# Weights stationary, input moving: one 512-column matmul over the input's high and low halves in place of two of 256 columns

## The chip, the cores and the metric

The kernel runs on one core of a Trainium2 chip. The metric is the device time of one execution in microseconds, given as the median of several runs. A core has a matrix engine (TensorE; PE in the profile, its weight loads PEld), a vector engine (VectorE, DVE), a scalar engine (ScalarE, ACT), GpSimd (POOL) and SyncE (SP), from whose queue the transfers from memory are issued here. Each engine works through its own list of instructions in order and waits for the others through semaphores. Matmul results are written to PSUM, which has eight banks of 512 float32 per partition; everything else lives in SBUF.

## The reference

One layer of a bidirectional encoder over 256 positions of width 2048. The input is normalised and multiplied by one wide matrix; its columns are cut into parts that feed two branches and their gates:

```python
h = _rms_norm(x, norm_g)
proj = jnp.einsum('bsd,dn->bsn', h, w_in.astype(h.dtype))
q_p, k_p, v_p, o_p, za_p, gif_p, xb_p, zb_p, ga_p, gb_p = jnp.split(proj, cuts, axis=-1)
ya = _mlstm_branch(q_p, k_p, v_p, o_p, za_p, gif_p, b_if, head_g)
yb = _rglru_branch(xb_p, zb_p, conv_w, conv_b, w_rg, b_rg, lam)
ya = jnp.einsum('bsw,wd->bsd', ya, w_branch_a.astype(ya.dtype))
yb = jnp.einsum('bsw,wd->bsd', yb, w_branch_b.astype(yb.dtype))
merged = (jax.nn.sigmoid(ga_p) * ya + jax.nn.sigmoid(gb_p) * yb).astype(x.dtype)
return x + jnp.einsum('bsd,de->bse', merged, w_out.astype(x.dtype))
```

A final normalisation follows. The first branch (mLSTM) has four heads with gated scores between queries and keys; the second (RG-LRU) has a short convolution along the sequence (the `xb` part), gates, and a linear recurrence run forwards and backwards; its result is multiplied by silu of the `zb` part.

## The kernel before

**High and low halves.** Every float32 operand of a large product is split in two: a high half, rounded to the matmul's input type (`F32R`), and a low half, the rounding's remainder. A product is then three matmuls: high by high, high by low, low by high. The normalised input (without its row factor, which is applied later: `rstd` as a column, `rbc` as a row) is held transposed, features on the partitions, as `hhi` (slot `H`) and `hlo` (slot `L`): 16 feature tiles of 256 positions each. `x_piece` (line 169) fills them two tiles at a time.

**Weights in chunks.** A block is 512 columns of a weight matrix, 2048 rows deep. It comes in eight chunks of 512 KB. `load_chunk` (line 96) issues the transfer on SP into one of five `raw` tiles, has ACT round it to `whi` (line 108, "the cast") and DVE subtract to get `wlo` (line 109, "the subtraction"). There are three pairs of `whi` and `wlo`, so the cast of a chunk can start when PE has finished the chunk three places before it.

**Two kinds of block.** `block_nat` (line 112) holds the input stationary and moves 512 columns of weights; its result has positions on the partitions. `block_tr` (line 128) holds 128 x 128 of the weights stationary and moves the input's 256 positions; its result has features on the partitions. For each of the 16 feature tiles k and each of four column groups m it issues three matmuls (lines 142 to 144): high weights by `hhi`, high weights by `hlo`, low weights by `hhi`. Two column groups share a bank, so a block fills a pair of banks; `pacc` has four single banks, so two pairs. `block_tr` serves 12 blocks: Q0, K0, Q1, K1 (the digit is the loop's index; K's results are also multiplied by `rbc`, line 388), XB0 to XB3 and ZB0 to ZB3. 31 blocks go through `block_nat`, three of them in the last projection.

**Order of the work.** Q0, K0, Q1, K1 come first. Then for each j in 0 to 3: `rg_block(j)` (XBj, its multiply by `rbc` into the padded tile `xp` on line 455, and the convolution on DVE on lines 461 to 468), followed by `head(j)` with three `block_nat` blocks V, O and Z. Then ZB0 to ZB3, then the gates and the branches' projections, and the output. Small steps hang in two queues. `tick()` (line 81), called ahead of each chunk, takes one step from each; `drain()` takes all that are left, `drain_to(fn)` all up to one step. In the queues are: the loads of x for the row factor (`r_load`), the row factor itself (`r_sum`, `r_row`, the latter a matmul of a diagonal and a copy to `rbc`), the gates (`g_...`), the score products (`s_mul`, `s_tr`), the recurrence's gate products (`unit`), exponentials (`decay`), roots (`root`) and scans (`scan`, lines 515 to 525), and a head's mixing and transposes (`mix`, `fin`). The steps of block XBj that are left after `head(j)` run during XB(j+1), those of XB3 during ZB0: one `root` and two `scan`.

A scheduler places the instructions on each engine's list from this order, with a cost model of its own. What stands under `urgent()` goes ahead of what doesn't: weight chunks and the emptying of PSUM are urgent, the convolution, scans, `fin` and `mix` are not.

## Time and profile before

| | |
|---|---|
| time, 3 runs | median 1053.61 us, 1052.96 to 1053.88 |
| span of the profiled execution, first to last instruction | 1050.9 us |
| mean granted TensorE clock of the span | 0.998 |
| transfers of weight chunks of `wi` | 255 of 512 KB and 2 of 256 KB |
| memory read and written | 196.32 MB, 2.10 MB; 189 GB/s over the span |
| GpSimd's busiest line, 673 (scales `fgs`, once) | 10.6 us |

The profile is of one execution; the runs' times are of others, and include what lies before the first and after the last instruction. The page gives the busy time of each engine as a share of the span, the chain of work that ended last, and groups of instructions by line. In a line of a group, the first number behind the bar is the group's busy time, the second the mean duration of one in ns, the last the time that the engine sat idle just before them, with what ended it. In a line of the timeline, the first number is the start in us from the span's start, the second the time to the end of the piece, then engine, line, operation, the tiles written and read, and how many instructions are merged in the piece; in brackets stands idle time before it. A matmul's duration includes the pipeline that it shares with its neighbours, so the distance between starts says what one costs. Windows give start and end, length, busy time of PE, PEld, DVE, ACT and POOL, clock, and what the transfers did.

### The profile page before, as it was taken

How to read it: one execution, taken by the hardware profiler on the slowest of the kernel's cores; microseconds unless marked ns; L12 is line 12 of the kernel's file. 1: busy time of each engine (PE TensorE's matmuls, PEld its weight loads, DVE VectorE, ACT ScalarE, POOL GpSimd, SP SyncE). 2: the span in 40 equal slices, each digit the busy share in tenths (PEclk: the TensorE clock that was granted, in tenths of full speed). 3: DMA queues.
4: the chain of work that ended last, by engine and by line, in shares of the span. 5: the costliest groups of instructions: out<-in, count | busy, mean ns of one | idle time of the engine just before them, and what ended most of it. 6: DMA issues, size and time to landing. Idle time of an engine off the chain costs nothing.

```text
span 1050.9 us, 14840 instructions
## 1 busy us (share of the span) xinstructions
PE 1039.4 (99%) x5876; PEld 914.9 (87%) x5876; DVE 646.9 (62%) x809; ACT 533.5 (51%) x689; POOL 36.7 (3%) x48
## 2 busy tenths in 40 slices
PE   9999999999999999999999999999999999999996
PEld 8999988898889888988999988888888888888886
DVE  6566785489549845974786654454454545545573
ACT  7535447765684658466644443434434344444461
POOL 2000000010001001000320000000000000000000
PEclk9999999999999999999999999999999999999999
DMA  9744545556655654664656556666666565667652
GB/s 339 254 158 143 180 159 185 163 182 198 196 161 167 198 197 160 187 214 161 200 181 184 180 194 195 191 197 191 191 199 192 190 186 188 192 194 261 198 201 80
DMA packets 55669, 199.39 MB, mean 190 GB/s; under 512 B 6192, under 2 KB 6448, under 8 KB 55216
## 3 DMA queue, kind: packets, MB, share of 16 engines
q1 hardware_dynamic: 55600, 198.44, 58.7%
q8 instruction: 46, 0.75, 0.3%
q14 instruction: 23, 0.19, 0.0%
HBM read 196.32 MB, written 2.10 MB: 189 GB/s over the span
## 4 chain that ended last, share of the span: by engine, by line
PE 97%; DVE 1%; issue 1%; DMA 0%; POOL 0%; POOLq 0%; ACT 0%; DVEq 0%; SPq 0%; ACTq 0%
PE acc L123 21%; PE acc L124 21%; PE acc L125 21%; PE acc L144 9%; PE acc L142 9%; PE acc L143 9%; PE aux L573 1%; PE aux L490 1%; PE aux L489 1%; PE aux L488 1%; PE aux L403 1%; DVE sC L522 1%; PE aux L708 0%; PE aux L709 0%; PE aux L285 0%
## 5 line engine op out<-in xcount | busy, mean ns | idle before, releaser
L109 DVE TENSOR_TENSOR wlo<-raw,whi 128x1024 fp32r<-128x1024 f32 (+1 forms) x345 | 420.6, 1220 | 354.3 <-ACT whi L108 353.8
L108 ACT CAST whi<-raw 128x1024 fp32r<-128x1024 f32 (+1 forms) x345 | 361.7, 1049 | 442.2 <-PE acc L125 302.7
L124 PE MATMUL acc<-wlo,sH 128*128 128x512 f32 x640 | 249.7, 390 | 0.0
L125 PE MATMUL acc<-whi,sL 128*128 128x512 f32 x640 | 249.4, 390 | 0.0
L123 PE MATMUL acc<-whi,sH 128*128 128x512 f32 x640 | 229.5, 390 | 0.0
L142 PE MATMUL acc<-sH,whi 128*128 128x256 f32 x768 | 218.4, 286 | 0.8 <-ACT whi L108 0.8
L143 PE MATMUL acc<-sL,whi 128*128 128x256 f32 x768 | 217.0, 284 | 0.0
L144 PE MATMUL acc<-sH,wlo 128*128 128x256 f32 x768 | 215.0, 285 | 1.3 <-DVE wlo L109 1.3
L142 PEld LDWEIGHTS acc<-sH,whi 128*128 128x128 f32 x768 | 148.0, 193 | 2.0 <-ACT whi L108 1.1
L143 PEld LDWEIGHTS acc<-sL,whi 128*128 128x128 f32 x768 | 148.0, 193 | 0.3
L144 PEld LDWEIGHTS acc<-sH,wlo 128*128 128x128 f32 x768 | 146.1, 192 | 2.2 <-DVE wlo L109 2.0
L125 PEld LDWEIGHTS acc<-whi,sL 128*128 128x128 f32 x640 | 120.2, 188 | 24.4
L124 PEld LDWEIGHTS acc<-wlo,sH 128*128 128x128 f32 x640 | 120.3, 188 | 23.7
L123 PEld LDWEIGHTS acc<-whi,sH 128*128 128x128 f32 x640 | 119.9, 188 | 24.1
L124 PE MATMUL acc<-wlo,sC 128*128 128x512 f32 x224 | 87.2, 389 | 0.0
L125 PE MATMUL acc<-whi,sD 128*128 128x512 f32 x224 | 87.2, 389 | 0.0
L123 PE MATMUL acc<-whi,sC 128*128 128x512 f32 x224 | 78.4, 389 | 0.0
L124 PE MATMUL acc<-wlo,sA 128*128 128x512 f32 x128 | 49.8, 389 | 0.0
L125 PE MATMUL acc<-whi,sB 128*128 128x512 f32 x128 | 49.8, 389 | 0.0
L125 PEld LDWEIGHTS acc<-whi,sD 128*128 128x128 f32 x224 | 42.1, 188 | 8.7
L124 PEld LDWEIGHTS acc<-wlo,sC 128*128 128x128 f32 x224 | 42.1, 188 | 8.6
L123 PEld LDWEIGHTS acc<-whi,sC 128*128 128x128 f32 x224 | 42.0, 188 | 8.7
(221 smaller groups left out, 859.3 us busy)
## 6 DMA issues: line engine op xcount, KB each, us to landing
raw<-wi SPq DMA_DIRECT2D x255, 512.0 KB, 3.6
raw<-wb SPq DMA_DIRECT2D x32, 512.0 KB, 4.2
raw<-wa SPq DMA_DIRECT2D x32, 512.0 KB, 3.5
raw<-wo SPq DMA_DIRECT2D x32, 512.0 KB, 3.5
raw<-wr SPq DMA_DIRECT2D x8, 512.0 KB, 4.4
sA<-xt SPq DMA_DIRECT2D x8, 256.0 KB, 7.2
sB<-x SPq DMA_DIRECT2D x4, 512.0 KB, 8.4
sA<-x SPq DMA_DIRECT2D x1, 2048.0 KB, 9.1
```

Source lines behind the costliest of these rows:

```text
L108: last_copy[0] = act.copy(hi[:, r], raw[:, r]).ins
L109: last_sub[0] = dve.tensor_sub(lo[:, r], raw[:, r], f(hi[:, r])).ins
L123: pe.matmul(ps[tb], a, wh, start=(k == 0), stop=False)
L124: pe.matmul(ps[tb], a, wl, start=False, stop=False)
L125: pe.matmul(ps[tb], b, wh, start=False, stop=(k == KT - 1))
L142: pe.matmul(dst, wh, a, start=first, stop=False, skip_group_check=True)
L143: pe.matmul(dst, wh, b, start=False, stop=False, skip_group_check=True)
L144: pe.matmul(dst, wl, a, start=False, stop=last, skip_group_check=True)
L403: pe.matmul(ps[:, tb * S:(tb + 1) * S], a, b, start=(n == 0), stop=(n == 5))
L488: pe.matmul(dst, whi[:, o:o + P], xh[:, r], start=True, stop=False)
L489: pe.matmul(dst, whi[:, o:o + P], xl[:, r], start=False, stop=False)
L490: pe.matmul(dst, wlo[:, o:o + P], xh[:, r], start=False, stop=True)
```

## The change

All `block_tr` blocks except Q0 get a new routine, `half_tr`. It computes half of a block (two column groups of 128) over all 16 feature tiles, from four chunks of 512 KB that hold four feature tiles of 256 columns each; the weights are laid out anew for that before the run (`_halves`). `hhi` and `hlo` now lie in one tile `HL`, with the 256 high and the 256 low columns of a feature tile side by side, so the first matmul moves 512 columns over both: its first 256 results are high by high, the next 256 high by low. The second matmul adds low weights by `hhi` to the first 256. A half block so fills a pair of banks, one bank for each column group. `pacc` has two tiles of two banks.

`fold` then adds the halves of both banks: ACT copies the second 256 columns of each into SBUF, DVE adds the first 256 to them. Behind it come the steps that were there before (multiply by `rbc`, split), which now read SBUF, and once for each half. In K0, `drain_to(r_row)` stands behind the first half, in ZB0 `drain()` behind the first half, in XB0 `drain()` behind both. Q0 keeps the three matmuls, under the name `block_first`. A scratch tile for the first matmuls and the last block's `H` and `L` slots are placed in other tiles of the same size.

```diff
+    def half_tr(src, half):
+        ps, both = acc_pair()
+        for kq in range(4):
+            tick()
+            hi, lo = load_chunk(src[half * 4 + kq])
+            for kk in range(4):
+                k = kq * 4 + kk
+                for m in range(2):
+                    o = kk * S + m * P
+                    pe.matmul(ps[m], hi[:, o:o + P], hl_t[:, 2 * k * S:2 * (k + 1) * S],
+                              start=(k == 0), stop=False, skip_group_check=True)
+                    pe.matmul(ps[m][:, :S], lo[:, o:o + P], hhi(k * S, (k + 1) * S),
+                              start=False, stop=(k == KT - 1), skip_group_check=True)
+        return both.rearrange("p (m q s) -> p m q s", m=2, q=2)
+
+    def fold(dst, both):
+        t = hp.tile([P, NB], F32, tag="fold", name=name("fold"), bufs=1)
+        t3 = t.rearrange("p (m s) -> p m s", m=2)
+        with urgent():
+            act.copy(t3, both[:, :, 1, :])
+            dst = t if dst is None else dst
+            dve.tensor_add(dst.rearrange("p (m s) -> p m s", m=2), both[:, :, 0, :], t3)
+        return dst
...
     def qk_block(blk, key, i, pre=()):
-        ps = block_tr(wi[blk], hhi, hlo, pre)
+        ps = block_first(wi[blk], hhi, hlo, pre) if pre else None
         for m in range(2):
             r = slice(m * NB, (m + 1) * NB)
-            v = ps[m]
+            if ps:
+                v = ps[m]
+            else:
+                v = hp.tile([P, 2 * NB], F32, tag="to" if m == 0 else "zz", name=name("kt"))[:, :NB]
+                fold(v, half_tr(wi[blk], m))
...
             if key[0] == "k":
                 if i == 1:
                     drain_to(r_row)
...
-        ps = block_tr(wi[BLK_XB + j], hhi, hlo)
-        if j == 0:
-            drain()
-            rg["hs"] = sl("E")
-        with urgent():
-            for i in range(2):
-                dve.tensor_mul(xp[:, 2 * i:2 * i + 2, 2:S + 2], ps[i].rearrange("p (n s) -> p n s", n=2), rbc2)
+        for i in range(2):
+            both = half_tr(wi[BLK_XB + j], i)
+            if j == 0 and i == 1:
+                drain()
+                rg["hs"] = sl("E")
+            v = fold(None, both)
+            with urgent():
+                dve.tensor_mul(xp[:, 2 * i:2 * i + 2, 2:S + 2], v.rearrange("p (n s) -> p n s", n=2), rbc2)
...
+        for i in range(2):
+            both = half_tr(wi[BLK_ZB + j], i)
+            if i == 0:
+                drain()
+                zt = hp.tile([P, 2 * NB], F32, tag="zz", name=name("zt"))
+                sg = hp.tile([P, 2 * NB], F32, tag="to", name=name("sg"))
+            v = zt[:, i * NB:(i + 1) * NB]
+            fold(v, both)
+            with urgent():
+                v3 = v.rearrange("p (m s) -> p m s", m=2)
+                dve.tensor_mul(v3, v3, rbc2)
```

More of the change, by code (lines that the diff above doesn't have):

```diff
@@ L44, in hybrid_encoder @@
     hp = ctx.enter_context(tc.tile_pool(name="hp", bufs=1))
-    pacc = ctx.enter_context(tc.tile_pool(name="pacc", bufs=4, space=bass.MemoryType.PSUM))
+    pacc = ctx.enter_context(tc.tile_pool(name="pacc", bufs=2, space=bass.MemoryType.PSUM))
     paux = ctx.enter_context(tc.tile_pool(name="paux", bufs=4, space=bass.MemoryType.PSUM))
@@ L63, in acc_pair @@
     def acc_pair():
-        return [pacc.tile([P, NB], F32, tag="acc", name=name("acc")) for _ in range(2)]
+        t = pacc.tile([P, 2 * NB], F32, tag="acc", name=name("acc"))
+        return [t[:, :NB], t[:, NB:]], t
     def urgent():
@@ L162, in hybrid_encoder, with hhi, hlo @@
     xs = sl("A")
-    hhi_t = sl("H", F32R)
-    hlo_t = sl("L", F32R)
-    hhi, hlo = Cols([hhi_t], 4096), Cols([hlo_t], 4096)
+    hl_t = sl("HL", F32R, 8192)
+    def hhi(a, b):
+        return hl_t[:, a + a // S * S:a + a // S * S + b - a]
+    def hlo(a, b):
+        return hl_t[:, a + a // S * S + S:a + a // S * S + S + b - a]
     xn = sl("B")
@@ L607, in hybrid_encoder @@
     for j in range(4):
-        ps = block_tr(wi[BLK_ZB + j], hhi, hlo)
-        drain()
-        zt = hp.tile([P, 2 * NB], F32, tag="zz", name=name("zt"))
-        sg = hp.tile([P, 2 * NB], F32, tag="to", name=name("sg"))
-        with urgent():
-            for i in range(2):
-                dve.tensor_mul(zt[:, i * NB:(i + 1) * NB].rearrange("p (m s) -> p m s", m=2),
-                               ps[i].rearrange("p (m s) -> p m s", m=2), rbc2)
+        for i in range(2):
[7 more added lines that the diff above has]
+            with urgent():
+                v3 = v.rearrange("p (m s) -> p m s", m=2)
+                dve.tensor_mul(v3, v3, rbc2)
         act.activation(sg, zt, AF.Sigmoid)
@@ L693, in hybrid_encoder @@
             out_piece(tb, j * NB, (j + 1) * NB, j, ps[tb])
-    lw = [sl(t, F32R) for t in ("H", "L", "E", "B")]
+    lw_t = sl("HL", F32R, 8192)
+    lw = [lw_t[:, :4096], lw_t[:, 4096:], sl("E", F32R), sl("B", F32R)]
     ch = []
@@ L739 @@
     w_in = a["w_in"][0]
+    wi = _chunks(np.concatenate([w_in[:, :8192], w_in[:, 8208:]], axis=1))
+    for lo, hi, a0 in ((BLK_Q + 1, BLK_V, 512), (BLK_XB, BLK_GA, 8208)):
+        wi[lo:hi] = _halves(w_in[:, a0:a0 + (hi - lo) * NB])
     cols = [v.reshape(-1, KT, P) for v in (a["norm_g"][0][None], a["head_g"][0][None], a["conv_b"][0][None],
```

22 lines of the change are left out of this document (12 added, 10 removed).

## The prediction

> **What bounds the kernel now.** I read the page first, for the engine that fills the span and for the chain of work that ended last.
>
> ```profile
> span 1050.9 us, 14840 instructions
> PE 1039.4 (99%) x5876; PEld 914.9 (87%) x5876; DVE 646.9 (62%) x809; ACT 533.5 (51%) x689; POOL 36.7 (3%) x48
> ...
> PE 97%; DVE 1%; issue 1%; DMA 0%; POOL 0%; POOLq 0%; ACT 0%; DVEq 0%; SPq 0%; ACTq 0%
> ...
> L142 PE MATMUL acc<-sH,whi 128*128 128x256 f32 x768 | 218.4, 286 | 0.8 <-ACT whi L108 0.8
> L143 PE MATMUL acc<-sL,whi 128*128 128x256 f32 x768 | 217.0, 284 | 0.0
> L144 PE MATMUL acc<-sH,wlo 128*128 128x256 f32 x768 | 215.0, 285 | 1.3 <-DVE wlo L109 1.3
> ```
>
> PE is busy for 1039.4 of 1050.9 us, and 97% of the chain is its own matmuls. The three lines that the change touches (142 to 144, 3 x 768 matmuls of 256 columns) waited 2.1 us in total for VectorE and ScalarE. So time here is PE time, and a matmul saved on PE is saved at the end, as long as the weights' halves arrive in time.
>
> The 286 ns are no price: matmuls overlap in the pipeline. The price is the distance between two starts, which the timeline of PE gives, first in the K block, then in a block of head 1 with 512 columns, then where the two kinds meet.
>
> ```profile
> 59.57 0.28 PE L143 MATMUL acc<-sL,whi 128*128 128x256 f32 x1
> ...
> 60.53 0.28 PE L142 MATMUL acc<-sH,whi 128*128 128x256 f32 x1
> ...
> 300.41 0.39 PE L123 MATMUL acc<-whi,sH 128*128 128x512 f32 x1
> ...
> 301.77 0.39 PE L123 MATMUL acc<-whi,sH 128*128 128x512 f32 x1
> ...
> 258.09 0.39 PE L123 MATMUL acc<-whi,sH 128*128 128x512 f32 x1
> 258.32 0.28 PE L489 MATMUL aux<-sD,rhi 128*128 128x256 f32 x1
> 258.43 0.28 PE L490 MATMUL aux<-sD,rlo 128*128 128x256 f32 x1
> ...
> 238.50 0.28 PE L144 MATMUL acc<-sH,wlo 128*128 128x256 f32 x1
> 238.62 0.63 PE L123 MATMUL acc<-whi,sH 128*128 128x512 f32 x2
> ```
>
> From 59.57 to 60.53 there are 8 steps: 0.120 us for 256 columns. From 300.41 to 301.77 there are 6: 0.2267 us for 512. Two of 256 cost 0.240, so each matmul carries a part of 0.0133 us that does not depend on its columns (0.240 - 0.2267). At the junctions both prices hold: a 512 is followed after 0.23, a 256 after 0.12.
>
> **The change part by part.** *Matmuls.* Of the 12 blocks with weights stationary (2 Q, 2 K, 4 XB, 4 ZB; 2304 / 12 = 192 matmuls each) the first Q block stays. In the other 11, each of 64 triples (16 k by 4 m) becomes a pair: 512 columns over hi and lo, then 256. That is 0.360 us against 0.2267 + 0.120 = 0.3467, 0.0133 us less, 704 times: **9.4 us off PE**. The 704 weight loads that go with them ran beside matmuls and free nothing more. A chunk of weights (8 pairs) takes 2.77 us instead of 2.88, a block 22.2 instead of 23.0, so the next chunk is needed up to 0.85 us earlier at a block's end.
>
> The Trainium skill, "TensorE: Matmul & The Clock Gate", section "Back-to-back issue gap", gives 2.5 ns as the part that does not depend on columns; by that the saving would be an estimated 704 x 2.5 ns = 1.8 us. The trace, at 13.3 ns, doesn't agree, and the sum goes by the trace.
>
> *The fold.* Each half block now ends in an ACT copy of one half of two banks, a DVE add of the other half, and then what was there before (a multiply by rbc, or the split). The nearest rows:
>
> ```profile
> L149 ACT CAST sC<-acc x4: 577/587/587, 30.7 to 84.6; 128x512 fp32r<-128x512 f32 x4
> ...
> L150 DVE TENSOR_TENSOR sD<-acc,sC x4: 675/692/693, 31.3 to 86.5; 128x512 fp32r<-128x512 f32 x4
> L150 DVE TENSOR_TENSOR sD<-kt,sC x4: 685/688/690, 57.7 to 114.5; 128x512 fp32r<-128x512 f32 x4
> ```
>
> So 22 copies of 0.59 us on ACT (13 us) and 22 adds of 0.69 on DVE (15 us). The multiply or split that follows reads SBUF instead of PSUM, 0.688 against 0.692: no change. PE doesn't wait for a fold: a half has its own pair of banks, and the pair is needed again only a half later, 11.1 us on. What the fold can do is hold up the weights' cast and subtraction queued behind it. The nearest case is the end of the first Q block, where two copies and two subtractions stand between chunks (ACT, DVE, then PE's first use of the chunk):
>
> ```profile
> 30.68 1.31 ACT L149 CAST sC<-acc 128x512 fp32r<-128x512 f32 x2 [1.23 <-PE acc L144]
> 31.88 1.05 ACT L108 CAST whi<-raw 128x1024 fp32r<-128x1024 f32 x1
> ...
> 32.97 1.23 DVE L109 TENSOR_TENSOR wlo<-raw,whi 128x1024 fp32r<-128x1024 f32 x1 [0.25 <-ACT whi L108]
> ...
> 37.44 0.28 PE L144 MATMUL acc<-sH,wlo 128*128 128x256 f32 x1
> ```
>
> The subtraction ends at 34.20, its chunk is used at 37.44: 3.2 us to spare. In Q1, both K blocks and ZB1 to ZB3 I therefore cost the folds at nothing; the three chunks in flight are the cover, and without it a fold would cost up to 0.6 + 0.7 us.
>
> *Where the cover is thin.* XB1 to XB3 and ZB0 carry the scans of the block before. The windows are XB1 and the V block behind it (PE, PEld, DVE, ACT busy); below them DVE and PE at the seam.
>
> ```profile
> 213.30:236.40 23.10, 23.10 (x189) 22.81 (x189) 21.58 (x26) 13.62 (x20) 4.48 (x6) 1.00 0.53 168
> 236.40:259.00 22.60, 22.60 (x114) 19.21 (x114) 21.69 (x36) 9.90 (x13) 0.00 (x0) 1.00 0.58 189
> ...
> 240.34 1.22 DVE L109 TENSOR_TENSOR wlo<-raw,whi 128x1024 fp32r<-128x1024 f32 x1
> 241.47 1.28 DVE L455 TENSOR_TENSOR xp<-acc,rbc 128x512 f32<-128x512 f32 x2
> 242.67 1.22 DVE L109 TENSOR_TENSOR wlo<-raw,whi 128x1024 fp32r<-128x1024 f32 x1
> ...
> 241.82 0.40 PE L124 MATMUL acc<-wlo,sH 128*128 128x512 f32 x1
> ```
>
> DVE is busy for 43.3 of 45.7 us, and the subtraction that ends at 241.56 is used at 241.82: 0.26 us to spare. The first half's fold now falls in the middle of XB1 and puts an add and a multiply (1.20 us for two, 241.47 to 242.67) ahead of that subtraction, and PE arrives 0.85 us sooner. If the order on DVE stayed, PE would stall 1.20 + 0.85 - 0.26 = 1.8 us, in each of three places. If scans and convolution, which are not urgent, give way, it stalls not at all. At the fourth place, behind ZB0, PE stalls already:
>
> ```profile
> 234.96 2.43 DVE L522 TENSOR_TENSOR_SCAN sC<-sC,sD 128x256 f32<-128x256 f32 x4
> ...
> 521.56 10.60 POOL L673 TENSOR_SCALAR sPT<-sPT 128x2048 f32<-128x2048 f32 x1 [4.40 <-DMA sPT<-fg]
> ...
> 522.29 1.22 DVE L515 SCALAR_TENSOR_TENSOR sD<-sC,sD 128x1024 f32<-128x1024 f32 x1
> ...
> 527.23 5.49 DVE L522 TENSOR_TENSOR_SCAN sC<-sC,sD 128x256 f32<-128x256 f32 x4
> 532.64 1.20 DVE L109 TENSOR_TENSOR wlo<-raw,whi 128x1024 fp32r<-128x1024 f32 x1
> ...
> 532.53 0.28 PE L143 MATMUL acc<-sL,whi 128*128 128x256 f32 x1
> 533.89 0.38 PE L144 MATMUL acc<-sH,wlo 128*128 128x256 f32 x1 [1.08 <-DVE wlo L109]
> ```
>
> The same scan that takes 2.43 us behind XB1 takes 5.49 while L673 runs on POOL; PE's next step is 1.36 us instead of 0.12, so 1.24 lost. This prices DVE work added to a full stretch: 3.06 us more there cost PE 1.24, four tenths. I take that share, between nothing and all: 0.4 x 1.20 = 0.5 us at each of four places, **2.0 us given back**. The earlier arrival I leave out of the chosen value, since the casts are released by PE and come earlier with it; it stays in the bound. Bounds: 1.24 us gained, if the stall behind ZB0 goes too, to 3 x 1.8 + (1.20 + 0.85) = 7.4 us lost.
>
> The Trainium skill, "SBUF — State Buffer", section "Who interferes with whom", says that a DVE instruction with two SBUF inputs contends with a GpSimd instruction that reads SBUF. The slow scan agrees (5.49 against 2.43 us); L515 at 522.29, with two such inputs as well, ran at its normal 1.22 and doesn't. By the rule the stall behind ZB0 would vanish if the new order moved the scans off L673, 1.24 us less in the sum.
>
> *What is moved.* In K0 the queue is now drained to r_row after the first half, and ZB0's queue after its first half.
>
> ```profile
> 31.20 0.28 PE L142 MATMUL acc<-sH,whi 128*128 128x256 f32 x1
> ...
> 42.14 0.28 DVE L270 TENSOR_SCALAR sE<-ident,rstd 128x128 f32<-128x128 f32 x1
> ...
> 509.40 0.28 PE L142 MATMUL acc<-sH,whi 128*128 128x256 f32 x1
> ...
> 518.17 0.74 DVE L581 SCALAR_TENSOR_TENSOR to<-aux,sq,zz 128x512 f32<-128x512 f32 x1
> ```
>
> K0 starts at 31.2, its first half ends near 42.3, and the diagonal that r_row multiplies is written at 42.42: r_row, in PE's order there, could hold PE 0.1 us, more if its x loads came later. The gate steps behind it come four chunks sooner; so do the score products, which were issued in a burst behind XB0. ZB0 starts near 509.4; the transposes drained after its first half (11.1 us later, 520.5) need what DVE finishes at 518.91. Both at nothing, 0 to 0.5 us. No DMA is added: a half block loads four chunks of the same 512 KB, in the same queue.
>
> Sum: 1053.61 - 9.4 + 2.0 = **1046.2 us**. Prices come from one profiled execution of span 1050.9; the median of the runs lies 2.7 us above, which is outside the first and last instruction and stays.
>
> **The rivals.** *Clean:* the new order puts scans and convolution behind the subtractions, no stall is added, or that behind ZB0 goes as well: 1053.6 - 9.4 = 1044.2, down to 1043.0. For it: 3 us to spare everywhere else. Against: DVE full for 45 us at a stretch.
>
> *DVE becomes the bound in XB1 to XB3 and ZB0:* all of the 7.4 us is paid, 1051.6. For it: 0.26 us to spare. Against: only the subtractions are wanted in time, and the chunks at the end of the V block had room again.
>
> *The pair doesn't save what it says:* the 13.3 ns belong to 256 columns rather than to a matmul. At 2.5 ns per matmul, 1.8 us saved and 2.0 given back: 1053.8. Against it stand the junction rows, and 0.2267 for 512 columns.
>
> *Slower:* ACT, strictly in order, reaches the fold's copy early and holds the casts behind it until PE ends the half. In the first Q block it waited 1.23 us so, harmless within 3.2 us to spare. From 3.2 us of waiting on, each further one is PE's; 22 halves at 0.52 us past that point eat 9.4 + 2.1 us and end at 1055.7. For it: 22 such waits in place of 11. Against: nothing in the trace comes near 3.2.
>
> **How the numbers follow.** A measurement of this kernel can tell about 0.2%, 2.1 us, from no change: 1051.5 to 1055.7 counts as the same. Forecast (1044.7 to 1048.5) 0.50; clean 0.27; DVE bound (1048.5 to 1052) 0.14; pair saves little 0.05; slower 0.04. Faster: 0.50 + 0.27 + 0.11 of the DVE case + 0.01 = 0.89; same 0.03 + 0.04 = 0.07; slower 0.04. The range 1043.0 to 1050.8 leaves out a few in 100 below and about 13 above.
>
> **What would show it.** Starts of the new lines: 0.227 from the 512 to the 256, 0.120 to the next. A half of 11.1 us. The V block behind XB1 to XB3 and the block behind ZB0 starting with PE gaps of some tenths of a us that wait for L109's successor. Wrong would be: a pair at 0.36; gaps at every half; ACT waiting for more than 3 us at a fold's copy with PE idle after it.

## The result, and the profile after

The changed kernel takes 1058.84 us (median of 4 runs, 1058.56 to 1060.04) against 1053.74 us (1052.96 to 1054.14) for the kernel before on the same chip: a ratio of 1.0053, 95% interval 1.0039 to 1.0068. It is 5 us slower, 12.6 us above the forecast and outside the range. The span of the profiled execution grew from 1050.9 to 1057.2 us.

The page of the kernel after, first the busy times, then the chain that ended last, then the groups of the pair (line 157 moves 512 columns, line 159 adds the 256 of the low weights; the subtraction is now line 110, the cast 109):

```profile
span 1057.2 us, 13470 instructions
...
PE 1037.9 (98%) x5172; PEld 877.0 (83%) x5172; DVE 660.5 (62%) x831; ACT 543.1 (51%) x711; POOL 26.8 (3%) x48
...
PE 90%; DVE 6%; issue 2%; ACT 1%; DMA 1%; SPq 0%; POOL 0%; POOLq 0%; DVEq 0%
...
L157 PE MATMUL acc<-sHL,whi 128*128 128x512 f32 x704 | 250.5, 398 | 0.0
...
L159 PE MATMUL acc<-sHL,wlo 128*128 128x256 f32 x704 | 199.7, 284 | 6.6 <-DVE wlo L110 6.5
```

704 matmuls are gone, as the change says. But VectorE, 1% of the chain before, now has 6% of it, and the low-weight matmul waits 6.6 us for the subtraction, where the waits of its predecessor were 1.3 us. The idle column doesn't hold all of it: the chunks that come late in a V block are on line 125.

Where the time went is seen by cutting the span at the first low-weight matmul of each block, in both profiles (in us; "forecast" is what the prediction's own terms make of each stretch):

| stretch | before | after | difference | forecast |
|---|---|---|---|---|
| up to K0 | 31.68 | 32.51 | +0.83 | 0 |
| K0, Q1, K1, XB0 | 108.41 | 107.35 | -1.06 | -3.4 |
| V0, O0, Z0 | 73.95 | 75.01 | +1.06 | 0 |
| XBj, Vj, Oj, Zj, j = 1 to 3 together | 293.79 | 299.77 | +5.98 | -1.1 |
| ZB0 | 26.05 | 28.60 | +2.55 | -0.4 |
| ZB1 to ZB3 | 69.38 | 66.56 | -2.82 | -2.5 |
| the rest | 447.66 | 447.39 | -0.27 | 0 |

The sum is +6.3, forecast was -7.4. The +1.06 of V0 to Z0 is mostly a shift: four matmuls of head 0's mixing (4 x 0.227 = 0.91 us), which stood behind XB1's first low-weight matmul, the cut, now stand ahead of it; in the later stretches that evens out, and ZB0 lost its four as well, so its true loss is 2.55 + 0.91 = 3.46 us. Most of the lost time is in XB1 to V3 and in ZB0, the stretches that the prediction called thin.

The first stall, in XB1: PE's timeline, then VectorE's just before it, both of the kernel after.

```profile
228.82 0.28 PE L159 MATMUL acc<-sHL,wlo 128*128 128x256 f32 x1
...
231.23 0.39 PE L159 MATMUL acc<-sHL,wlo 128*128 128x256 f32 x1 [1.24 <-DVE wlo L110]
```

```profile
222.90 0.75 DVE L616 SCALAR_TENSOR_TENSOR to<-aux,sq,zz 128x512 f32<-128x512 f32 x1 [1.00 <-POOL sq L615]
...
226.50 2.43 DVE L555 TENSOR_TENSOR_SCAN sE<-sC,sE 128x256 f32<-128x256 f32 x4
228.84 1.20 DVE L110 TENSOR_TENSOR rlo<-raw,rhi 128x1024 fp32r<-128x1024 f32 x1
229.96 1.22 DVE L110 TENSOR_TENSOR wlo<-raw,whi 128x1024 fp32r<-128x1024 f32 x1
...
233.36 0.68 DVE L169 TENSOR_TENSOR fold<-acc,fold 128x512 f32<-128x512 f32 x1
```

The subtraction that PE waits for ends at 231.18. Ahead of it, back to back, are a scan (2.43 us) and a subtraction for the gates' weights; the first fold (line 169) comes only at 233.36, *after* the stall. So it is not the fold's own 0.68 us that stands in the way here. The kernel before has the same three in the same order:

```profile
225.04 2.42 DVE L520 TENSOR_TENSOR_SCAN sE<-sC,sE 128x256 f32<-128x256 f32 x4
227.38 1.20 DVE L109 TENSOR_TENSOR rlo<-raw,rhi 128x1024 fp32r<-128x1024 f32 x1
228.50 1.22 DVE L109 TENSOR_TENSOR wlo<-raw,whi 128x1024 fp32r<-128x1024 f32 x1
```

In the kernel after each starts 1.46 us later, although XB1 itself starts 0.31 us earlier (213.50 against 213.81): the delay was there before the scan, and p1 below shows where such a delay can come from. From 223 us on VectorE has no idle time, and in the windows (start, end, length, then busy PE, PEld, DVE, ACT, POOL, clock, transfers) the second half of the stretch is full:

```profile
213.30:237.50 24.20, 22.96 (x132) 19.76 (x131) 21.83 (x25) 14.05 (x21) 2.87 (x6) 1.00 0.51 160
237.50:262.00 24.50, 24.16 (x114) 19.63 (x114) 24.09 (x40) 12.39 (x18) 0.00 (x0) 1.00 0.59 193
```

24.09 of 24.50 us on DVE; PE has 1.24 and 0.34 us idle. In ZB0 the stall is larger. VectorE, GpSimd, PE, and windows of the same kernel:

```profile
521.58 4.68 DVE L550 SCALAR_TENSOR_TENSOR sD<-sC,sD 128x1024 f32<-128x1024 f32 x1
526.18 1.21 DVE L551 TENSOR_TENSOR sE<-sE,sC 128x1024 f32<-128x1024 f32 x1
527.32 1.21 DVE L110 TENSOR_TENSOR wlo<-raw,whi 128x1024 fp32r<-128x1024 f32 x1
```

```profile
520.89 6.02 POOL L711 TENSOR_SCALAR sPT<-sPT 128x2048 f32<-128x2048 f32 x1 [0.31 <-DMA sPT<-fg]
```

```profile
525.58 0.28 PE L159 MATMUL acc<-sHL,wlo 128*128 128x256 f32 x1
528.59 0.39 PE L159 MATMUL acc<-sHL,wlo 128*128 128x256 f32 x1 [2.49 <-DVE wlo L110]
```

```profile
528.60:530.00 1.40, 1.40 (x8) 1.26 (x9) 1.40 (x2) 0.00 (x0) 1.34 (x2) 0.95 0.41 64
530.00:531.00 1.00, 1.00 (x5) 0.81 (x4) 1.00 (x3) 0.00 (x0) 0.80 (x2) 0.50 0.88 352
531.00:532.00 1.00, 1.00 (x5) 0.90 (x4) 1.00 (x3) 0.00 (x0) 0.00 (x0) 0.50 0.21 82
532.00:533.00 1.00, 1.00 (x3) 0.44 (x2) 1.00 (x2) 0.56 (x1) 0.00 (x0) 0.50 0.00 0
...
534.00:536.00 2.00, 2.00 (x13) 1.72 (x11) 2.00 (x4) 0.01 (x1) 0.00 (x0) 1.00 0.78 252
```

One instruction of VectorE took 4.68 us instead of 1.22 while GpSimd's line 711 ran, PE stood for 2.49 us, and then the granted clock fell to 0.50 for about 3 us: 5, 5 and 3 matmuls in a microsecond, 13 in two once the clock is back. PE looks busy in those windows; only the clock column and the counts tell.

The saving itself is there. PE in ZB1 and ZB2, and in K0:

```profile
564.14 0.39 PE L157 MATMUL acc<-sHL,whi 128*128 128x512 f32 x1
...
565.18 0.39 PE L157 MATMUL acc<-sHL,whi 128*128 128x512 f32 x1
...
32.99 0.40 PE L157 MATMUL acc<-sHL,whi 128*128 128x512 f32 x1
...
35.81 0.40 PE L157 MATMUL acc<-sHL,whi 128*128 128x512 f32 x1
```

Three pairs from 564.14 to 565.18 are 0.3467 us each, the forecast to the nanosecond; ZB2 takes 22.19 us where it took 23.04. But in K0 eight pairs from 32.99 to 35.81 are 0.3525 each. Over all pairs that follow each other without a stall or a foreign matmul between, the mean is 0.350.

### The profile page after: what moved, and what is told of

Read it like the earlier page. It is cut to its first block, busy times and chain, and to the rows that moved or that the text cites. A ratio compares the mean times of both kernels' runs of the same rounds, so it can differ in the third digit from the quotient of the medians.

```text
span 1057.2 us, 13470 instructions
## 1 busy us (share of the span) xinstructions
PE 1037.9 (98%) x5172; PEld 877.0 (83%) x5172; DVE 660.5 (62%) x831; ACT 543.1 (51%) x711; POOL 26.8 (3%) x48
## 4 chain that ended last, share of the span: by engine, by line
PE 90%; DVE 6%; issue 2%; ACT 1%; DMA 1%; SPq 0%; POOL 0%; POOLq 0%; DVEq 0%
PE acc L125 21%; PE acc L126 21%; PE acc L124 21%; PE acc L157 13%; PE acc L159 7%; DVE wlo L110 2%; PE aux L608 1%; DVE sC L557 1%; PE aux L525 1%; PE aux L524 1%; PE aux L523 1%; PE acc L145 1%; DMA raw<-wi 1%; PE acc L144 1%; PE acc L143 1%
## 5 line engine op out<-in xcount | busy, mean ns | idle before, releaser
L125 PE MATMUL acc<-wlo,sHL 128*128 128x512 f32 x640 | 250.5, 391 | 1.0 <-DVE wlo L110 1.0
L157 PE MATMUL acc<-sHL,whi 128*128 128x512 f32 x704 | 250.5, 398 | 0.0
L124 PE MATMUL acc<-whi,sHL 128*128 128x512 f32 x640 | 249.8, 390 | 0.0
L126 PE MATMUL acc<-whi,sHL 128*128 128x512 f32 x640 | 249.5, 390 | 0.0
L159 PE MATMUL acc<-sHL,wlo 128*128 128x256 f32 x704 | 199.7, 284 | 6.6 <-DVE wlo L110 6.5
L157 PEld LDWEIGHTS acc<-sHL,whi 128*128 128x128 f32 x704 | 132.7, 188 | 30.3
L125 PEld LDWEIGHTS acc<-wlo,sHL 128*128 128x128 f32 x640 | 120.3, 188 | 26.7 <-DVE wlo L110 3.6
L159 PEld LDWEIGHTS acc<-sHL,wlo 128*128 128x128 f32 x704 | 133.6, 190 | 9.2 <-DVE wlo L110 8.5
L124 PEld LDWEIGHTS acc<-whi,sHL 128*128 128x128 f32 x640 | 120.3, 188 | 24.8
L126 PEld LDWEIGHTS acc<-whi,sHL 128*128 128x128 f32 x640 | 120.2, 188 | 24.0
L124 PE MATMUL acc<-whi,sA 128*128 128x512 f32 x128 | 49.8, 389 | 0.0
L124 PEld LDWEIGHTS acc<-whi,sA 128*128 128x128 f32 x128 | 24.0, 188 | 5.0
```

What stands on the lines that cost most here:

```text
L124: pe.matmul(ps[tb], a, wh, start=(k == 0), stop=False)
L125: pe.matmul(ps[tb], a, wl, start=False, stop=False)
L126: pe.matmul(ps[tb], b, wh, start=False, stop=(k == KT - 1))
L157: pe.matmul(ps[m], hi[:, o:o + P], hl_t[:, 2 * k * S:2 * (k + 1) * S], start=(k == 0), stop=False, skip_group_check=True)
L159: pe.matmul(ps[m][:, :S], lo[:, o:o + P], hhi(k * S, (k + 1) * S), start=False, stop=(k == KT - 1), skip_group_check=True)
```

## The experiments

Each kernel was run beside the kernel before; ratios are to it, with 95% intervals. The stretches in the table at the end of this section are read from the profiles in the same way as the stretches above.

**e1_no_fold**: the changed kernel without the fold; the consumers read the first 256 columns of each bank directly, so the second 256 (the term high weights by low input) are left out.

```diff
-            act.copy(t3, both[:, :, 1, :])
-            dst = t if dst is None else dst
-            dve.tensor_add(dst.rearrange("p (m s) -> p m s", m=2), both[:, :, 0, :], t3)
-        return dst
+            pass
+        return both[:, :, 0, :]
```

> Leaves out the fold (22 ACT copies and 22 DVE adds), and with it the term high weights by low input in 11 blocks; the steps behind it read the first 256 columns of each bank from PSUM. Theory A (VectorE is full in XB1 to XB3, the V blocks behind them and ZB0, and the fold's adds there put the weights' subtractions behind PE's need): the PE gaps that wait for the subtraction in those blocks, 2.3 us for each of three and 4.9 us around ZB0 in the changed kernel, fall below 0.5 us each, and the time to 1046 to 1050 us. Theory B (the fold is innocent; half blocks, the drains that were moved and the pace of the pair cost the time): the gaps stay and the time is over 1055 us.

Measured: 1059.39 us (1058.78 to 1059.98), ratio 1.006 [1.0045, 1.0075]. The stalls stay: 1.22 and 0.65 us in XB1 and V1, 2.49 in ZB0. 22 copies and 22 adds less change nothing that can be measured, so the fold alone is not the cause.

**e2_selective**: the changed kernel with XB0 to XB3 and ZB0 back on three matmuls of 256 and a whole block each, without a fold.

```diff
-            both = half_tr(wi[BLK_XB + j], i)
...
-            v = fold(None, both)
+        ps = block_first(wi[BLK_XB + j], hhi, hlo)
```

> XB0 to XB3 and ZB0 go back to three matmuls of 256 columns with the old layout and drains; K0, Q1, K1 and ZB1 to ZB3 keep the pair and the fold. Theory A: gaps as before the change (1.2 us behind ZB0, under 0.2 in XB1 to XB3), six blocks save up to 0.85 us each, less what a slower pace of the pair takes in K0 to K1: 1048.5 to 1051 us. Theory B: the pair's pace and the moved steps in K0 to K1 eat the gain; 1053 us or more.

Measured: 1056.93 us (1055.69 to 1057.13), ratio 1.0034 [1.0022, 1.0046]. With the loops of before in exactly the thin places, XB1 to XB3 still stall 0.62 us each and ZB0 2.35 (the profile is of its quickest run, 1055.69). What is left of the change in these blocks is the PSUM tile of two banks, the hunk that the prediction passed over; the pairs in K0, Q1 and K1 are left too, so the tile is a suspect here and not yet shown.

**p1_before_pairs**: the kernel before, with that hunk alone.

```diff
-    pacc = ctx.enter_context(tc.tile_pool(name="pacc", bufs=4, space=bass.MemoryType.PSUM))
+    pacc = ctx.enter_context(tc.tile_pool(name="pacc", bufs=2, space=bass.MemoryType.PSUM))
...
-        return [pacc.tile([P, NB], F32, tag="acc", name=name("acc")) for _ in range(2)]
+        t = pacc.tile([P, 2 * NB], F32, tag="acc", name=name("acc"))
+        return [t[:, :NB], t[:, NB:]]
```

> The kernel before with one thing of the change alone: the pair of PSUM banks is one tile of two banks, in place of two tiles of one bank. No matmul is changed and no fold is added. Theory C (the shared tile is the cause: readers on two engines are ordered per tile, so where a block's two banks are emptied by ScalarE and then VectorE, as in Q, V and Z, ScalarE's read of the second bank now waits for VectorE's read of the first; the order of both engines' lists changes with it, and the weights' subtractions come late in XB1 to XB3 and ZB0): 1055 to 1059 us, with PE gaps of 0.7 us or more that wait for the subtraction in XB1 to XB3. Theory B (half blocks, moved drains and the pair's pace are the cause): 1052 to 1054 us.

Measured: 1059.25 us (1059.05 to 1059.93), ratio 1.0056 [1.0041, 1.0071]. No pair, no fold, no half block, and 6 us slower: as much as the whole change. In XB1 PE waits again for the subtraction:

```profile
235.53 0.39 PE L145 MATMUL acc<-sH,wlo 128*128 128x256 f32 x1 [1.00 <-DVE wlo L110]
```

The mechanism can be read where a Z block is emptied (ScalarE's sigmoid of two banks, VectorE's product of each bank with its sigmoid). First ScalarE and VectorE of the kernel before, then of p1:

```profile
214.06 1.26 ACT L557 ACTIVATE zz<-acc,rstd 128x512 f32<-128x512 f32 x2
...
214.77 1.28 DVE L558 TENSOR_TENSOR zz<-zz,acc 128x512 f32<-128x512 f32 x2 [0.77 <-ACT zz L557]
216.09 1.23 DVE L559 TENSOR_TENSOR zz<-zz,to 128x1024 f32<-128x1024 f32 x1
```

```profile
216.93 0.69 ACT L558 ACTIVATE zz<-acc,rstd 128x512 f32<-128x512 f32 x1
217.52 1.04 ACT L109 CAST whi<-raw 128x1024 fp32r<-128x1024 f32 x1
218.45 0.69 ACT L558 ACTIVATE zz<-acc,rstd 128x512 f32<-128x512 f32 x1
...
217.65 0.69 DVE L559 TENSOR_TENSOR zz<-zz,acc 128x512 f32<-128x512 f32 x1 [0.78 <-ACT zz L558]
218.59 1.23 DVE L110 TENSOR_TENSOR wlo<-raw,whi 128x1024 fp32r<-128x1024 f32 x1 [0.25 <-ACT whi L109]
219.73 0.68 DVE L559 TENSOR_TENSOR zz<-zz,acc 128x512 f32<-128x512 f32 x1
```

With two tiles the two sigmoids run back to back and the two products behind them. With one tile the second sigmoid stands behind the first product: in the traces of p1 and of the kernel after, the semaphore that releases it is the one that VectorE's products raise, and it starts at 218.45, behind the product's end at 218.34; in the kernel before it is PE's, as for the first sigmoid. ScalarE and VectorE then hand each other turns, a cast and a subtraction slip between, and the last product ends at 220.41 - 216.93 = 3.5 us after the first sigmoid began, instead of 216.05 - 214.06 = 2.0. The chain behind it (heads' norm, products, scans) reaches VectorE later, in the stretch in which it has nothing to spare. A reordered list of instructions is what the run shows; that each microsecond of the 6 comes by this one wait is not shown, since the planner (the scheduler that lays out the engines' lists) placed both engines' instructions anew: the lists in the two traces differ in about 100 places on ScalarE and 160 on VectorE.

**f1_single_banks**: the changed kernel with single banks back, and the fold done per bank.

```diff
-        t = pacc.tile([P, 2 * NB], F32, tag="acc", name=name("acc"))
-        return [t[:, :NB], t[:, NB:]], t
+        t = [pacc.tile([P, NB], F32, tag="acc", name=name("acc")) for _ in range(2)]
+        return t, t
```

> The changed kernel with PSUM tiles of one bank again; the fold is done bank by bank (two ScalarE copies and two VectorE adds of 256 columns in place of one of each of 512). Theory C: the gaps in XB1 to XB3 shrink to under 0.5 us each, 1046 to 1051 us, although the fold costs more instructions. Theory B: 1056 us or more.

Measured: 1058.79 us (1056.38 to 1059.08), ratio 1.0046 [1.0031, 1.0061]. Undoing what costs 6 us by itself gives nothing back. The stalls only moved: 1.35, 1.15 and 1.37 us at the starts of V1, V2 and V3, and 4.46 in ZB0.

**f4_single_no_fold**: f1 without the fold as well (again the second 256 columns are not added).

```diff
-        return both[:, :, 0, :]
+        return [both[m][:, :S] for m in range(2)]
```

> Neither the shared PSUM tile nor the fold: tiles of one bank, and the steps behind a half block read the first 256 columns of each bank (leaves out the term high weights by low input in 11 blocks). So far each of the two alone, and both together, end near 1059 us. Theory D (both draw on one reserve, the spare time of the weights' subtractions on a full VectorE, and either alone uses it up): with neither, the PE gaps in XB1 to XB3 fall below 0.5 us each and the time to 1046 to 1052 us, the rest being the gaps around ZB0, whose drain still stands behind the first half. Theory B (half blocks by themselves, emptied twice as often, are enough): gaps over 1 us stay in XB1 to XB3 and the time over 1055.

Measured: 1059.49 us (1058.71 to 1060.26), ratio 1.0061 [1.0044, 1.0078]. That was a miss for theory D: with neither of the two suspects, XB1 to XB3 still stall 1.3 us each, in two gaps, and ZB0 4.84. What is left is the half block (its pace and its order) itself. The next two runs take pace and order apart.

**h6_before_pace**: the kernel before, with the faster pace alone, made by leaving out 32 columns of one matmul in three.

```diff
-                    pe.matmul(dst, wh, b, start=False, stop=False, skip_group_check=True)
+                    c = S if pre else 224
+                    pe.matmul(dst[:, :c], wh, b[:, :c], start=False, stop=False, skip_group_check=True)
```

> The kernel before, with the second of the three matmuls (high weights by the low input) cut from 256 to 224 columns in the 11 blocks behind Q0; it leaves those 32 columns' low term out, so its output lacks it. Each triple should cost 0.0133 us less (32/256 of 0.120 is 0.0150), the pair's saving, with no half block, no fold, no shared tile and nearly the order of before on ACT and DVE. Theory A (the full VectorE can't follow a faster PE): gaps appear in front of the low-weight matmuls behind XB1 to XB3 and in ZB0, and the gain of 704 x 0.0133 = 9.4 us is cut to 0 to 5 us: 1048 to 1053. Theory B (the gaps need a changed order: half blocks, the emptying in the middle of a block): no new gaps, 1043 to 1045.

Measured: 1049.57 us (1048.96 to 1050.06), ratio 0.9965 [0.9951, 0.9979]. Where weights come early, it gains: 2.53 us in K0 to XB0, and 1.40 us in ZB2 and ZB3, that is 10.9 ns for each of 128 triples. In XB1 to Z1 it gains nothing: 97.95 us against 97.93, and the later two are at 98.17 and 98.21. There a faster PE only meets VectorE sooner. Behind ZB0 PE stalls 1.74 us (1.08 before), and ZB0 and ZB1 together take 0.7 us more. So with nearly the order of before and three pairs of weight tiles, nothing of the saving arrives in these four blocks.

**h5_half_old_pace**: f4 with three matmuls of 256 into the same columns, so the order of half blocks without the pace.

```diff
+                    pe.matmul(ps[m][:, :S], hi[:, o:o + P], hhi(k * S, (k + 1) * S),
+                              start=(k == 0), stop=False, skip_group_check=True)
+                    pe.matmul(ps[m][:, :S], hi[:, o:o + P], hlo(k * S, (k + 1) * S),
+                              start=False, stop=False, skip_group_check=True)
```

> Half blocks on single banks with no fold, but three matmuls of 256 columns into the same 256 columns of PSUM in place of the pair: the whole product is computed, at the old pace of 0.360 us for a triple. Theory A (pace): the gaps behind XB1 to XB3 go away, each of these three stretches takes 97.9 us as before, total 1052 to 1055. Theory B (order): the gaps of 0.6 to 1.4 us stay although PE is no faster than before; with no saving against them the time is 1060 to 1068.

Measured: 1060.25 us (1059.75 to 1061.0), ratio 1.0069 [1.0054, 1.0084]. Stretches of 99.19 to 99.23 us instead of 97.93, although PE is no faster; f4, with the pace, has 99.2 to 99.5. The length is nearly the same with a fast and a slow PE: it is VectorE's, which has no idle time from 222 us to the stall. Its list ahead of the stall in V1 shows what stands in the way:

```profile
231.21 0.75 DVE L500 TENSOR_TENSOR xp<-acc,rbc 128x256 f32<-128x256 f32 x2
...
240.31 1.21 DVE L570 TENSOR_TENSOR sE<-sE,sC 128x1024 f32<-128x1024 f32 x1
241.45 0.73 DVE L506 TENSOR_SCALAR sD<-xp,pks 128x256 f32<-128x256 f32 x2
242.09 1.22 DVE L110 TENSOR_TENSOR wlo<-raw,whi 128x1024 fp32r<-128x1024 f32 x1
```

```profile
243.36 0.50 PE L125 MATMUL acc<-wlo,sHL 128*128 128x512 f32 x1 [0.69 <-DVE wlo L110]
```

Line 500 is the multiply that empties XB1's first half, now in the middle of the block, as the prediction said. Line 506 is the convolution's first step: half of XB1 is emptied 11 us earlier, so the convolution can start earlier, and the planner puts two of its steps ahead of a subtraction that has no such time. In the kernel before, that subtraction starts at 240.34, straight behind the recurrence's product, and here at 242.09. Of the 1.75 us, 0.44 are there already at the scan (225.48 against 225.04), 0.67 are the first half's multiply (231.21 to 231.88) and 0.64 the two steps (241.45 to 242.09). The gap is 0.69 us.

Over the kernel, 3.8 of the 7 us lie in the three stretches. The other 3.3 lie in ZB0 and ZB1, where this kernel has the early drain too (a gap of 3.05 us, and half the clock after it); there it doesn't tell the two apart.

**e3_late_drain**: the changed kernel with ZB0's queue emptied after the second half instead of the first.

```diff
-            if i == 0:
+            if j == 0 and i == 0:
+                t0 = xp[:, :2, 2:S + 2]
+                with urgent():
+                    act.copy(t0, both[:, :, 1, :])
+                    dve.tensor_add(t0, both[:, :, 0, :], t0)
+                continue
+            if i == 0 or j == 0:
                 drain()
```

> The changed kernel with ZB0's drain behind the second half (the first half's sum waits in the convolution's padded tile, which is free by then). If the early drain, which puts both scans and the last transposes of the head in front of the second half's weights, makes the 5 us of gaps around ZB0, they fall to 1 to 2.5 us, and the time to 1055 to 1057. If they come from VectorE being full whatever the order, the time stays within 1 us of 1058.8.

Measured: 1058.7 us (1058.52 to 1058.87), ratio 1.0051 [1.0036, 1.0066]: the same time. In ZB0 the first gap shrinks from 2.49 to 1.35 us, the clock stays at 1.00 and the block takes 26.80 us instead of 28.60; but ZB1 gets a gap of 1.04. In that profile ZB2 starts 1.3 us less late than in the changed kernel's, but ZB2 and ZB3 then run at 22.61 us each instead of 22.19, the pair's slower pace, which takes 0.85 of it back. The median shows none of it.

**e5_pair_order**: both 512s of a feature tile first, then both 256s.

```diff
                     pe.matmul(ps[m], hi[:, o:o + P], hl_t[:, 2 * k * S:2 * (k + 1) * S],
                               start=(k == 0), stop=False, skip_group_check=True)
+                for m in range(2):
+                    o = kk * S + m * P
                     pe.matmul(ps[m][:, :S], lo[:, o:o + P], hhi(k * S, (k + 1) * S),
```

> The changed kernel with the order within a feature tile 512, 512, 256, 256 in place of 512, 256, 512, 256. It asks where the pace of the pair comes from, which the changed kernel shows as 0.3467 us in some half blocks and 0.353 in others. If a 256 behind a 512 sets it, half as many such steps leave half of the loss: 0.350 in the slow half blocks and 1 to 1.5 us off the time. If it is a matter of the phase in which PE's list runs, the pace stays mixed and the time within 1 us of 1058.8.

Measured: 1058.82 us (1057.03 to 1060.61), ratio 1.0051 [1.0036, 1.0066]. The pace becomes even, 348.4 ns a pair in all blocks, and K0 to XB0 take 106.16 us instead of 107.35; the stalls take it back.

**e6_four_bufs** and **e7_before_four_bufs**: four pairs of `whi` and `wlo` and three `raw` tiles, in the kernel after and in the kernel before.

```diff
-    def load_chunk(src, dst=None, tag="w", bufs=3, parts=1):
+    def load_chunk(src, dst=None, tag="w", bufs=4, parts=1):
         with urgent():
-            raw = wp.tile([P, KC * NB], F32, tag="raw", name=name("raw"), bufs=5)
+            raw = wp.tile([P, KC * NB], F32, tag="raw", name=name("raw"), bufs=3)
```

> The changed kernel with four pairs of high and low weight tiles in place of three, and three raw tiles in place of five (the same memory). Theory A: a fourth pair lets the cast and the subtraction start a chunk (2.7 us) sooner, so part of VectorE's backlog is covered: the gaps in XB1 to XB3 fall from 2.3 to under 1 us each, time 1050 to 1055 us. Theory B: no change beyond 1 us (1058 to 1060). If three raw tiles starve the transfers, both are slower; the next run shows that.

> The kernel before the change with the same four pairs and three raw tiles: the control of the run above. Theory A: it loses at most the 1.2 us gap behind ZB0, 1052 to 1054 us. Over 1055 would say that three raw tiles starve the transfers.

Measured: e6 1050.92 us (1048.94 to 1051.5), ratio 0.9975 [0.9966, 0.9985]; e7 1051.93 us (1051.67 to 1052.37), ratio 0.9986 [0.9977, 0.9996]. A chunk of slack turns the change from 5 us slower into 1 us faster than its counterpart. The gaps of XB1 to XB3 are gone; ZB0 keeps 1.68 and 0.52, and ZB0 and ZB1 together take no less than in the kernel after (51.28 against 50.78).

**h7_pairs_four**: p1 with the same four pairs.

> The kernel before with the PSUM tile of two banks (the 6 us slower one of p1_before_pairs) and four pairs of weight tiles with three raw tiles. If the shared tile costs its time only by making subtractions late, the deeper weights take the gaps of 1.0 to 1.4 us in XB1 to XB3 away: 1051.5 to 1054. If it costs time in another way as well, 1056 or more.

Measured: 1051.93 us (1051.61 to 1052.65), ratio 0.999 [0.9981, 1.0]: the time of e7. So what the shared tile costs goes through weights that come late; with weights a chunk further ahead it is free.

**f2_single_four**, **g1_late_single_four**, **g2_late_order**: f1 with four pairs; that with the late drain of e3; that with the order of e5. Their edits are those shown.

> The run above with four pairs of weight tiles and three raw tiles as well. Theory C: what gaps are left behind ZB0 shrink too, 1043 to 1049 us. Theory B: as the changed kernel with four pairs, 1050 to 1052.

> PSUM tiles of one bank, four pairs of weight tiles, three raw tiles (1047.5 us so far, with one gap of 1.5 us in ZB0), and ZB0's drain behind the second half. If that gap is the early drain's, it goes: 1045 to 1046.5 us. If not, 1047 to 1048.

> The run above with the order 512, 512, 256, 256 in a feature tile, which in the changed kernel gave one pace of 0.3484 us per pair in all blocks, in place of 0.3467 in some and 0.353 in others. With few gaps left to take it back, the mean pace should show: 0.35 to 0.3484 over 704 pairs is 1 us, so 1044 to 1046; no change against the run above would say that the pace isn't on the path.

Measured: f2 1047.52 us (1046.96 to 1048.72), ratio 0.9947 [0.993, 0.9964], with one gap left, 1.32 us in ZB0. g1 1046.36 us (1045.82 to 1048.0), ratio 0.9936 [0.9922, 0.9951], with no gap over 0.2 us. g2 **1044.45 us** (1043.94 to 1044.86), ratio 0.9915 [0.9901, 0.993]: 8.5 us below the median of the kernel before on that chip (1052.9), the fastest of all. Against g1 it gains 1.9 us where 1 was expected, 1.44 of them in K0 to XB0 (106.17 us against 107.61): without stalls the pace is on the path. Its page:

```profile
span 1042.7 us, 13554 instructions
...
PE 1031.9 (99%) x5172; PEld 875.3 (84%) x5172; DVE 660.9 (63%) x853; ACT 546.2 (52%) x733; POOL 33.9 (3%) x48
...
PE 96%; issue 1%; DMA 1%; DVE 1%; SPq 0%; ACT 0%; POOL 0%; POOLq 0%; DVEq 0%
...
L161 PE MATMUL acc<-sHL,wlo 128*128 128x256 f32 x704 | 139.6, 279 | 0.0
```

VectorE has as much to do as in the kernel after (660.9 against 660.5 us), and the low-weight matmuls wait for nothing.

All kernels in one table (us; the stretch is XB1 to Z1, the first of three that differ by at most 0.5):

| kernel | pairs of weight tiles | half blocks | fold | two-bank tile | faster pace | stretch | ZB0 + ZB1 | median |
|---|---|---|---|---|---|---|---|---|
| before | 3 | | | | | 97.93 | 49.37 | 1052.9 to 1053.7 |
| h6 | 3 | | | | yes | 97.95 | 50.06 | 1049.57 |
| p1 | 3 | | | yes | | 99.87 | 49.47 | 1059.25 |
| e2 | 3 | in part | in part | yes | in part | 98.93 | 49.61 | 1056.93 |
| h5 | 3 | yes | | | | 99.19 | 52.65 | 1060.25 |
| f4 | 3 | yes | | | yes | 99.47 | 53.39 | 1059.49 |
| f1 | 3 | yes | yes | | yes | 99.01 | 53.84 | 1058.79 |
| e1 | 3 | yes | | yes | yes | 99.87 | 51.25 | 1059.39 |
| after | 3 | yes | yes | yes | yes | 99.95 | 50.78 | 1058.84 |
| e3 | 3 | yes | yes | yes | yes | 99.94 | 49.52 | 1058.70 |
| e5 | 3 | yes | yes | yes | yes | 99.26 | 53.73 | 1058.82 |
| e7 | 4 | | | | | 97.91 | 49.69 | 1051.93 |
| h7 | 4 | | | yes | | 97.89 | 49.46 | 1051.93 |
| e6 | 4 | yes | yes | yes | yes | 97.53 | 51.28 | 1050.92 |
| f2 | 4 | yes | yes | | yes | 97.37 | 49.61 | 1047.52 |
| g1 | 4 | yes | yes | | yes | 97.37 | 48.27 | 1046.36 |
| g2 | 4 | yes | yes | | yes | 97.16 | 48.39 | 1044.45 |

Read down: with three pairs, the kernels whose edits lay out VectorE's and ScalarE's lists anew end at 1058.7 to 1060.3, with one such edit or with several; only e2, which has the old loops in the thin blocks, lies lower, at 1056.93. With four, the stretch comes down to 97.16, near the 97.93 - 0.85 = 97.08 of a PE that never waits.

## Why the prediction was wrong

**What bounds the kernel now** was read from the share of the span, 97% of the chain on PE. That holds on average. In XB1 to V1 PE and VectorE were both at their limit, with 0.26 us between them; the prediction saw the number and still counted the saving of these blocks in full. h6 shows that it didn't arrive there: nothing of the 0.85 us forecast for XB1.

**The pair's 13.3 ns** was right as a price: 22.19 us in ZB1 to ZB3, by the pitch of 0.3467 us. Its size over all 704 was too large by 704 x 3.4 ns = 2.4 us, since most halves up to ZB0 ran at 0.3525 to 0.354. In K0 to XB0, 1.06 of the 3.4 us arrived; the slower pace accounts for some 1.1 of the missing 2.3, the rest isn't traced. The rival "the pair saves little" (2.5 ns) falls.

**Where the cover is thin** is the step that failed, the 2.0 us given back. It priced the fold's 1.20 us added to an otherwise unchanged list, taken at four tenths. Measured, XB1 to ZB0 lost 5.98 + 3.46 = 9.4 us where 1.4 were to be gained (4 x (0.85 - 0.5)). With the 3.4 us that the pairs of these four blocks were to save, that is 12.8 us given back instead of 2.0, over the bound of 7.4 as well. The fold's own instructions weren't what did it: without them (e1, f4) the time is the same. What did it was the planner's new order, and two parts of the change each bring such an order by themselves: the shared PSUM tile sends the emptying of Z to and fro between two engines (p1, +6 us), and half blocks put the first half's multiply and two convolution steps ahead of a subtraction (h5, +7 us, with the early drain). That multiply is the one of these that the prediction had priced. Its remark, that PE stalls not at all if "scans and convolution, which are not urgent, give way", left it to the planner to keep the subtractions in time; with three pairs and a new order it never did. The bound was worked out with the old order, and so was too low. How the 12.8 us divide among the parts is not shown, since taking out one or two of them (e1, f1, f4) leaves the time as it is; that the part in XB1 to Z3 goes through late weights is shown by the fourth pair (e6, h7). ZB0 and ZB1 keep theirs in e6 (51.28 us) and lose it only with single banks and the late drain as well (g1, 48.27).

**The two-bank tile** stands in the diff, and the prediction put no price on it. Tracking by tile makes two engines that read different banks of it wait for each other. By itself it costs 6 us (p1), though undoing it alone (f1) gains nothing.

**What is moved, at nothing:** ZB0's early drain wasn't free in the profile. With it three steps of the recurrence (lines 550, 550, 551) stand between the subtractions at 519.3 and 527.32, without it (e3) two (550, 551; the subtraction comes at 526.2). One of them is held for over 4 us beside GpSimd's instruction in both kernels, so that is not the drain's doing; but the later subtraction makes PE's gap 1.14 us longer, and behind it the clock falls, which it doesn't in e3. Late, the block is 1.8 us shorter (e3), but ZB1 and the pace of ZB2 and ZB3 take most of it back and the median doesn't move; with four pairs g1's median is 1.2 us below f2's, with runs that overlap. Its worth stays open.

**The rivals.** "DVE becomes the bound in XB1 to XB3 and ZB0" was the mechanism, at 0.14 and with 1051.6 too small. "Slower", by ScalarE held at a fold's copy, didn't happen: in the kernel after each of the 22 copies starts straight behind a cast, without idle time on ScalarE, and e1 has no such copy and the same time.

**The last term of the sum** was misread without harm: of the 2.7 us between the span and the median, only some 1.9 lie outside the first and last instruction (in the kernel after 1059.12 us against a span of 1057.2); the rest is one execution against others.

**Still open:** why the medians of p1, h5, f1, f4 and after lie so close together, what sets the two paces of the pair, and the 0.83 us lost up to K0 (in the profile of the kernel after the granted clock is 0.50 for 3.4 us from 7.6 us on, but p1 loses 1.0 us there without that). No run changed the order alone, for instance by holding the convolution back with three pairs; that would be the direct test.

## What to carry to other kernels

Where two engines run full side by side, a gain on one isn't a gain, and the reserve between them (here 0.26 us) is the number to price a change against: an edit that makes the planner lay out the lists again can use it up, even one that adds no work. Look for the reserve's depth first (one more pair of weight tiles, at the price of two raw ones, turned 5 us slower into 2 faster, and 6 faster with the shared tile undone), and then make the change. Joining two PSUM banks in one tile is an edit of its own: count who reads each half, and in which order.

## What the runs showed of the hardware

**Two paces of one pair.** 512 then 256 columns alternating run at 0.3467 us a pair (0.230 and 0.117) or at 0.3525 to 0.354, either for many pairs on end; the mode often changes at a foreign matmul or a stall. Sorted as 512, 512, 256, 256 they ran at 0.3484 in every block.

**The clock after a short gap.** PE's gap of 2.49 us in the kernel after was followed by about 3 us at a granted clock of 0.50, and so were gaps of 1.74 (h6), 2.49 (e1) and 3.05 us (h5). Around gaps of 2.73 (e5), 4.46 (f1) and 4.84 us (f4) the clock was at 0.50 for about 7 us. Gaps of 1.68 (e6) and 2.35 us (e2) had no such spell. The Trainium skill, "TensorE: Matmul & The Clock Gate", section "HAM oscillation — how this bites in real kernels", puts the rule at gaps of over some 3.4 us; here 1.74 us was once enough, so a gap that seems too short can cost twice. The column ZB0 + ZB1 of the table holds such a spell in h6, h5, f4, f1, e1, e5 and after, and none in the others.

**One VectorE instruction beside GpSimd.** In the kernel before it was a scan (its four pieces 5.49 us instead of 2.43), in the kernel after a two-input product (4.68 instead of 1.22), in p1 a subtraction (4.53 instead of 1.22):

```profile
522.19 4.53 DVE L110 TENSOR_TENSOR wlo<-raw,whi 128x1024 fp32r<-128x1024 f32 x1
```

One stretch of 3.1 to 3.5 us is lost each time, whatever stands there, and the held instruction ends 0.7 us (after, p1) or 1.2 us (before) ahead of the end of GpSimd's (526.26 and 526.91 in the kernel after). The Trainium skill, "SBUF — State Buffer", section "Who interferes with whom", says that the two contend for one read interface when the VectorE instruction has two SBUF inputs; all three have, and so far the trace agrees. But in the kernel before four others with two such inputs, from 522.29 us on, ran at their normal 1.22 us beside the same GpSimd instruction, so which one is held isn't explained. What it costs depends on the reserve behind it: PE then stood for 1.08 us in the kernel before (a scan held), 2.49 in the kernel after (a product), 0.21 in p1 (a subtraction itself), and not at all in g2, where a subtraction took 4.61 us and a fourth pair was in stock.
